# Token-shift mixes built in PSUM instead of SBUF, and all their low parts on VectorE

## The chip, the cores and the metric

The kernel runs on one core of a Trainium2 chip. The metric is the device time of one launch, in microseconds (us). A run before the change takes 3714.47 us, the median of three. TensorE (PE), VectorE (DVE), ScalarE (ACT), GpSimd (POOL) and SyncE (SP, which here only issues DMAs) run side by side and meet through semaphores.

## The reference

The program is a two-layer encoder trunk over 1024 tokens of width 1024: layer 0 is attention, layer 1 an RWKV-7 time mixing, and each layer has a squared-ReLU MLP. The change lies at the start of layer 1:

```python
dx_p = jnp.pad(h, ((0, 0), (1, 0), (0, 0)))[:, :-1] - h      # previous token minus this one
dx_n = jnp.pad(h, ((0, 0), (0, 1), (0, 0)))[:, 1:] - h       # next token minus this one
def mix(c):
    return h + dx_p * mu_prev[c] + dx_n * mu_next[c]
xw, xa, xg = mix(1), mix(4), mix(5)
r = mix(0) @ w_r
k = mix(2) @ w_k
v = mix(3) @ w_v
# and, for each direction d: tanh(xw @ w1[d]), xa @ a1[d], sigmoid(xg @ g1[d])
```

A mix is thus a weighted sum of a token and its two neighbours, with weights per channel; six mixes feed six groups of projections.

## The kernel before

Layer 1's input lies in SBUF as `u` (channels on partitions in 8 tiles `kt`, tokens along the free dimension, one column of zeros at either end). Work goes by halves of 512 tokens. Products are made in three passes of a split format: each operand is cut into a high part (fp32r) and a low part (what is left), and `mm3` multiplies high by high, high by low and low by high into one PSUM bank. So each `mix` of one channel tile and one half (128 x 512) is five instructions:

1. ACT writes `x = u * c0` (L884), c0 being one minus both weights;
2. and 3. DVE adds the previous and the next token, each times its weight, in place in `x` (L886, two instructions);
4. ACT rounds `x` to the high part `xh` (L890; the tile is `xmh` or `xsh`);
5. DVE, or POOL for c = 5 and c = 1, subtracts: `xl = x - xh` (L891).

`x` comes from pool `p0`, three buffers in SBUF. `stream` runs over the 8 channel tiles: a mix, the load of the weight tile `wr`, its high part on ACT (L904), its low part on POOL (L905), then the matmuls. `together` takes turns between streams. The stage that the change touches is the block under `es_h`. For each half it runs the first four output tiles of r beside the gate's hidden layer (c = 5), then the other four (which use the same mixes, kept in `px`) beside the hidden layers of c = 1 and c = 4. That is 4 x 8 mixes a half, 64 in all, and 576 matmuls of 512 columns. The projections of k and v (c = 2 and c = 3) follow under `es_a` and after it, with 32 more mixes, beside work of the second low-rank layers.

The kernel uses PSUM as 8 banks of 128 x 512 f32. In the `es_h` stage four belong to `r_pm` (r's sums) and one each to `s0` and `s1` (the hidden layers' sums); two are free. Before the stage all 8 banks are the MLP's ring `pm` (six in a left-hand pool, two in a right-hand one, taken in turn; the MLP's last transposes use it too). After it, `es_a` takes four banks (`s0` three, `s1` one).

A scheduler of the framework orders the instructions of each engine when the program is built, by the order in which they are written and by what its own clock says is ready; each engine then runs its list strictly in order. Nothing in the stage is ordered by hand.

## Time and profile before

| | |
|---|---|
| median of 3 runs | 3714.47 us (3712.27 to 3717.64) |
| the profiled execution: time, span | 3712.8 us, 3710.7 us |
| PE, DVE, ACT, POOL busy, share of the span | 86%, 70%, 50%, 50% |
| mean granted clock of TensorE | 0.904 |

The time of the profiled execution is 2.1 us above its span, which runs from the first to the last instruction. A busy share is a mean over stages that have different limits, so the stage has to be read by itself. Matmuls overlap one another, so that the sum of their times is more than the time that they need.

### The profile page before, as it was taken

How to read it: one execution, taken by the hardware profiler on the slowest of the kernel's cores; microseconds unless marked ns; L12 is line 12 of the kernel's file. 1: busy time of each engine (PE TensorE's matmuls, PEld its weight loads, DVE VectorE, ACT ScalarE, POOL GpSimd, SP SyncE). 2: the span in 40 equal slices, each digit the busy share in tenths (PEclk: the TensorE clock that was granted, in tenths of full speed). 3: DMA queues.
4: the chain of work that ended last, by engine and by line, in shares of the span. 5: the costliest groups of instructions: out<-in, count | busy, mean ns of one | idle time of the engine just before them, and what ended most of it. 6: DMA issues, size and time to landing. Idle time of an engine off the chain costs nothing. (4 is left out here: it accounts for less than half of the span.)

```text
span 3710.7 us, 61321 instructions
## 1 busy us (share of the span) xinstructions
PE 3197.8 (86%) x22168; PEld 2599.8 (70%) x22168; DVE 2596.9 (70%) x4617; ACT 1854.2 (50%) x4244; POOL 1850.4 (50%) x1642
## 2 busy tenths in 40 slices
PE   7999989799998978878888687787787889999998
PEld 6788987688777755555566575666666667887776
DVE  3355564744599979986963678888886565449996
ACT  2366564455543345654533365556566445554333
POOL 1000001655598877754566434444331146558887
PEclk9999999899999989879987587788787899999999
DMA  6222224232322032248766444444443413223023
GB/s 199 71 78 88 70 74 153 92 118 103 108 91 114 12 127 74 82 143 230 230 209 189 112 111 112 111 122 120 119 109 114 137 65 148 106 80 142 28 87 114
DMA packets 425100, 425.70 MB, mean 115 GB/s; under 512 B 138667, under 2 KB 338475, under 8 KB 418652
## 3 DMA queue, kind: packets, MB, share of 16 engines
q1 hardware_dynamic: 423612, 417.58, 36.3%
q0 software_dynamic: 1184, 4.20, 0.4%
q8 instruction: 174, 2.85, 0.3%
q14 instruction: 130, 1.06, 0.1%
HBM read 290.83 MB, written 138.20 MB: 116 GB/s over the span
## 5 line engine op out<-in xcount | busy, mean ns | idle before, releaser
L101 PE MATMUL pm<-bhi,lo 128*128 128x512 f32 x840 | 333.1, 399 | 46.3 <-DVE lo L130 46.1
L130 DVE TENSOR_TENSOR lo<-x,hi 128x512 fp32r<-128x512 f32 x300 | 322.1, 1080 | 61.8 <-ACT hi L129 61.7
L129 ACT ACTIVATE hi<-x 128x512 fp32r<-128x512 f32 x300 | 189.6, 633 | 323.4 <-DVE x L127 126.5
L100 PE MATMUL pm<-blo,hi 128*128 128x512 f32 x840 | 331.8, 395 | 8.6 <-POOL blo L130 8.1
L99 PE MATMUL pm<-bhi,hi 128*128 128x512 f32 x840 | 320.5, 394 | 5.4 <-ACT bhi L129 5.0
L127 POOL TENSOR_TENSOR x<-w1r 128x512 f32<-128x512 f32 x160 | 214.0, 1341 | 202.1 <-DVE lo L130 178.1
L130 POOL TENSOR_TENSOR blo<-bx,bhi 128x512 fp32r<-128x512 f32 x138 | 222.3, 1612 | 26.6 <-ACT bhi L129 26.0
L1270 POOL TENSOR_TENSOR af<-af,amask 128x512 f32<-128x512 f32 x128 | 163.8, 1286 | 136.7 <-ACT af L1269 111.9
L101 PEld LDWEIGHTS pm<-bhi,lo 128*128 128x128 f32 x840 | 158.4, 189 | 99.1 <-DVE lo L130 67.6
L905 POOL TENSOR_TENSOR wl<-wr,wh 128x512 fp32r<-128x512 f32 (+2 forms) x144 | 188.8, 1322 | 77.1 <-ACT wh L904 57.1
L1266 PE MATMUL A<-zr,bk 128*128 128x128 f32 x1024 | 187.4, 346 | 44.3 <-DVE bk L1259 38.1
L127 POOL TENSOR_TENSOR bx<-w 128x512 f32<-128x512 f32 x140 | 215.5, 1541 | 9.5
L886 DVE SCALAR_TENSOR_TENSOR x<-u,mu,x 128x512 f32<-128x512 f32 x192 | 208.4, 1121 | 7.9 <-ACT x L884 5.7
L1266 PEld LDWEIGHTS A<-zr,bk 128*128 128x128 f32 x1024 | 166.5, 249 | 58.6 <-POOL bk L1260 21.0
L127 DVE TENSOR_TENSOR x<-h 128x512 f32<-128x512 f32 x140 | 195.5, 1408 | 5.3 <-ACT h L268 2.7
L100 PEld LDWEIGHTS pm<-blo,hi 128*128 128x128 f32 x840 | 159.0, 189 | 49.5 <-POOL blo L130 16.0
L99 PEld LDWEIGHTS pm<-bhi,hi 128*128 128x128 f32 x840 | 159.3, 190 | 38.9 <-ACT bhi L129 5.9
L99 PE MATMUL mm<-xmh,wh 128*128 128x512 f32 x384 | 168.5, 460 | 17.0 <-ACT xmh L890 6.5
L1418 PE MATMUL c<-af,sv 128*64 128x64 f32 x1024 | 97.5, 275 | 79.8 <-DVE h L1412 71.2
L100 PE MATMUL mm<-xml,wh 128*128 128x512 f32 x384 | 157.1, 412 | 7.6 <-DVE xml L891 7.6
L1412 DVE SCALAR_TENSOR_TENSOR h<-c,pc,hd 64x64 f32<-64x64 f32 x448 | 126.8, 283 | 47.9 <-PE c L1403 30.3
L583 ACT ACTIVATE S<-S,mneg 128x256 f32<-128x256 f32 (+2 forms) x256 | 125.2, 501 | 67.0 <-DVE mneg L578 44.1
(370 smaller groups left out, 10044.3 us busy)
## 6 DMA issues: line engine op xcount, KB each, us to landing
w1r<-in_mlp_w_dram SPq DMA_DIRECT2D x32, 1024.0 KB, 5.4
w<-in_mlp_w_dram SPq DMA_DIRECT2D x32, 1024.0 KB, 5.5
x<-x SPq DMA_DIRECT2D x64, 386.0 KB, 3.4
hd<-h SPq DMA_DIRECT2D x24, 1024.0 KB, 4.2
h<-hd SPq DMA_DIRECT2D x24, 1024.0 KB, 7.8
wr<-in_w_rkv_dram SPq DMA_DIRECT2D x96, 256.0 KB, 2.8
rk<-rk SPq DMA_DIRECT2D x64, 256.0 KB, 3.9
x<-cs SPq DMA_DIRECT2D x32, 260.0 KB, 3.9
```

The source lines that it names most:

```text
L99: nc.tensor.matmul(out, lhsT=ahi, rhs=bhi, start=start, stop=False)
L100: nc.tensor.matmul(out, lhsT=ahi, rhs=blo, start=False, stop=False)
L101: nc.tensor.matmul(out, lhsT=alo, rhs=bhi, start=False, stop=stop)
L127: add.tensor_tensor(out=y, in0=x, in1=blocks[term[2]], op=ALU.add if term[1] == "+" else ALU.subtract)
L129: nc.scalar.activation(hi, x, AF.Copy)
L130: sub.tensor_tensor(out=lo, in0=x, in1=hi, op=ALU.subtract)
L583: nc.scalar.activation(s[:, :n], s[:, :n], AF.Exp, bias=mneg[:, i:i + 1], scale=-1.0)
L886: nc.vector.scalar_tensor_tensor(out=x, in0=at(2 * i), scalar=mu[:, i, c, kt:kt + 1], in1=x, op0=ALU.mult, op1=ALU.add)
L905: nc.gpsimd.tensor_tensor(out=wlo, in0=wr, in1=whi, op=ALU.subtract)
L1266: nc.tensor.matmul(ps[:, fsl(u, P)], lhsT=bk[:, u, j].rearrange("p a b -> p (a b)"), rhs=zr[:, u].rearrange("p a b -> p (a b)"), start=Tru ...
L1270: nc.gpsimd.tensor_tensor(out=o, in0=o, in1=consts["amask"].unsqueeze(1).to_broadcast([P, 4, P]), op=ALU.mult)
L1412: nc.vector.scalar_tensor_tensor(out=hn[rows, cols], in0=ch[rows, 128:192], scalar=pc[rows, u:u + 1], in1=hd[rows, cols], op0=ALU.mult, op ...
```

## The change

For the `es_h` stage alone, `x` is a PSUM tile: a pool of two banks is opened with `s0` and `s1`, and removed from the table before the stages of k and v, whose mixes find the SBUF pool `p0` again. And the subtraction that makes the low part is on DVE for every mix; c = 5 and c = 1 (32 of the 64 mixes) had it on POOL. The arithmetic is the same.

```diff
@@ mix
-            x = p0.tile([P, 512], F32, tag="x", name="x")
+            x = psd.get("x", p0).tile([P, 512], F32, tag="x", name="x")
             nc.scalar.activation(x, at(1), AF.Copy, scale=c0[:, c, kt:kt + 1])
...
-            (nc.gpsimd if c in (5, 1) else nc.vector).tensor_tensor(out=xl, in0=x, in1=xh, op=ALU.subtract)
+            nc.vector.tensor_tensor(out=xl, in0=x, in1=xh, op=ALU.subtract)
@@ under es_h
-            psd.update({n: pool(f"r_p{n}", 1, st=es_h, space=PSUM) for n in ("s0", "s1")})
+            psd.update({n: pool(f"r_p{n}", b, st=es_h, space=PSUM) for n, b in (("s0", 1), ("s1", 1), ("x", 2))})
             for half in range(2):
                 together(main(0, 0, half, 0, r_done(half)), gate_hidden(5, half))
                 together(main(0, 0, half, 1, r_done(half)), hidden(1, 0, half), hidden(4, 1, half))
+            del psd["x"]
```

## Rows read from the trace of the kernel before

**Rows 1.** The page: the span, then busy time, share and instructions of each engine.

```profile
span 3710.7 us, 61321 instructions
PE 3197.8 (86%) x22168; PEld 2599.8 (70%) x22168; DVE 2596.9 (70%) x4617; ACT 1854.2 (50%) x4244; POOL 1850.4 (50%) x1642
```

**Rows 2.** Busy time of each engine from 1381 to 1588 us, the stage of the change (the end of the MLP's last tiles at its left edge): stretch, its length, PE, weight loads, DVE, ACT, POOL (busy us, instructions), granted clock, DMA share, GB/s.

```profile
1381.00:1588.00 207.00, 162.09 (x592) 115.74 (x592) 197.50 (x182) 124.21 (x237) 148.88 (x117) 0.90 0.25 82
```

**Rows 3.** DVE's groups in the same stretch: line, operation, shapes, count, busy us, mean ns of one, idle before them and what ended it.

```profile
L886 DVE SCALAR_TENSOR_TENSOR x<-u,mu,x 128x512 f32<-128x512 f32 x132 | 147.5, 1160 | 7.2 <-ACT x L884 5.7
L891 DVE TENSOR_TENSOR xml<-x,xmh 128x512 fp32r<-128x512 f32 x16 | 20.9, 1308 | 0.2
L891 DVE TENSOR_TENSOR xsl<-x,xsh 128x512 fp32r<-128x512 f32 x16 | 17.9, 1132 | 0.0
L988 DVE TENSOR_TENSOR sg<-th,sg 128x512 fp32r<-128x512 f32 x4 | 4.8, 1207 | 0.1
...
L976 DVE CAST ta<-th 64x512 fp32r<-64x512 f32 x2 | 0.8, 422 | 0.0
```

**Rows 4.** L886, and L891 on DVE with `xml` as its output, over the whole span: count, then the shortest, median and longest in ns, first and last start.

```profile
L886 DVE SCALAR_TENSOR_TENSOR x<-u,mu,x x192: 719/833/1852, 1381.2 to 1943.9; 128x512 f32<-128x512 f32 x192
L891 DVE TENSOR_TENSOR xml<-x,xmh x48: 676/693/1786, 1390.4 to 1946.5; 128x512 fp32r<-128x512 f32 x48
```

**Rows 5.** Timelines of DVE and of POOL around 1445 us: start, length, what.

```profile
1443.65 0.74 DVE L886 SCALAR_TENSOR_TENSOR x<-u,mu,x 128x512 f32<-128x512 f32 x1
1444.31 0.68 DVE L988 TENSOR_TENSOR sg<-th,sg 128x512 fp32r<-128x512 f32 x1
...
1446.47 1.68 DVE L988 TENSOR_TENSOR sg<-th,sg 128x512 fp32r<-128x512 f32 x1
...
1444.41 1.74 POOL L905 TENSOR_TENSOR wl<-wr,wh 128x512 fp32r<-128x512 f32 x1 [2.15 <-DVE x L886]
1446.12 1.48 POOL L891 TENSOR_TENSOR xsl<-x,xsh 128x512 fp32r<-128x512 f32 x1
```

**Rows 6.** A stretch of layer 0's MLP, 1100 to 1300 us. First the engines' busy times as in rows 2; then L335, whose second input `pm` is a PSUM bank (shortest, median, longest); then a group of the same stretch with both inputs in SBUF.

```profile
1100.00:1300.00 200.00, 180.04 (x771) 143.01 (x771) 199.31 (x201) 75.56 (x131) 169.41 (x110) 1.00 0.15 58
L335 DVE TENSOR_TENSOR acc<-acc,pm x92: 672/674/677, 1099.6 to 1288.3; 128x512 f32<-128x512 f32 x92
L130 DVE TENSOR_TENSOR lo<-x,hi 128x512 fp32r<-128x512 f32 x44 | 62.3, 1431 | 0.0
```

**Rows 7.** Scalar-tensor-tensor instructions of DVE over the whole span: L1047 with its second tensor `sm` in PSUM, L806 with its first in PSUM (`mm`) and with both in SBUF (`y`), and L73, which is 1024 wide (shortest, median, longest).

```profile
L1047 DVE SCALAR_TENSOR_TENSOR kk<-k,par,sm x16: 733/734/748, 1641.0 to 1878.1; 128x512 f32<-128x512 f32 x16
L806 DVE SCALAR_TENSOR_TENSOR y<-mm,prs,grow x24: 740/743/752, 604.8 to 3012.8; 128x512 f32<-128x512 f32 x24
L806 DVE SCALAR_TENSOR_TENSOR y<-y,prs,grow x8: 743/744/752, 588.4 to 2941.0; 128x512 f32<-128x512 f32 x8
L73 DVE SCALAR_TENSOR_TENSOR un<-xt,rs,ngrow x8: 1283/1284/1286, 18.0 to 80.0; 128x1024 f32<-128x1024 f32 x8
```

**Rows 8.** How closely such instructions follow one another: DVE's timeline at 1641 us (start, length), and one piece of the chain that ended last, six instructions of L335 in a row.

```profile
1640.96 0.74 DVE L1047 SCALAR_TENSOR_TENSOR kk<-k,par,sm 128x512 f32<-128x512 f32 x1
1641.62 0.75 DVE L886 SCALAR_TENSOR_TENSOR x<-u,mu,x 128x512 f32<-128x512 f32 x1
...
3409.85 3.58 DVE acc L335 x6
```

**Rows 9.** ACT's groups from 1381 to 1588 us, as in rows 3.

```profile
L884 ACT ACTIVATE x<-u,c 128x512 f32<-128x512 f32 x64 | 45.3, 720 | 33.5 <-POOL xsl L891 12.8 <-DVE xml L891 11.7 <-DVE xsl L891 8.8
L890 ACT ACTIVATE xsh<-x 128x512 fp32r<-128x512 f32 x48 | 30.1, 628 | 26.6 <-DVE x L886 26.3
L904 ACT ACTIVATE wh<-wr 128x512 fp32r<-128x512 f32 x33 | 20.4, 619 | 5.2 <-PE mm L100 4.4 <-DMA wr<-in_w_rkv_dram 0.8
L904 ACT ACTIVATE wh<-wr 128x128 fp32r<-128x128 f32 x32 | 9.6, 298 | 0.5 <-POOL wl L905 0.3 <-PE mm L100 0.2
L904 ACT ACTIVATE wh<-wr 128x256 fp32r<-128x256 f32 x16 | 6.5, 405 | 0.0
```

**Rows 10.** PE: the first and the last of 26 matmuls in a row (start, length), and what PE's idle time before the stage's matmuls ended with, from 1381 to 1588 us (us, times).

```profile
1396.11 0.39 PE L99 MATMUL mm<-xmh,wh 128*128 128x512 f32 x1
...
1401.88 0.40 PE L100 MATMUL mm<-xsl,wh 128*128 128x512 f32 x1
  DVE xsl L891: 18.5, 13
  POOL wl L905: 14.0, 23
...
  DVE xml L891: 11.9, 8
```

**Rows 11.** The edges of the stage. ACT's timeline: the last copies of the MLP's transposes out of its PSUM banks (L837) and the stage's first writes of `x`; PE's timeline: a wait at the first matmuls; and the first matmul of `es_a` into its own banks, over the whole span.

```profile
1375.77 0.59 ACT L837 ACTIVATE u<-pm 128x512 f32<-128x512 f32 x1
1378.25 1.95 ACT L884 ACTIVATE x<-u,c 128x512 f32<-128x512 f32 x3
1393.97 0.59 ACT L837 ACTIVATE u<-pm 128x512 f32<-128x512 f32 x1
1394.61 0.19 PEld L99 LDWEIGHTS mm<-xmh,wh 128*128 128x128 f32 x1 [1.54 <-ACT u L837]
L1088 PE MATMUL sm<-sg,g2h x64: 388/396/796, 1608.4 to 1910.0; 128*128 128x512 f32 x64
```

## The prediction, made before the change was run

> **What bounds the kernel now.** I read the page's first part for the whole [rows 1], then only the stage of the change, because a share of the span says nothing about a stage. From 1381 to 1588 us DVE is busy 197.5 of 207.0 us; PE's 162.1 us are overlapped matmuls, ACT has 124.2 and POOL 148.9 [rows 2]. PE's need is smaller than it looks: 26 matmuls start between 1396.11 and 1401.88 us, 0.231 us apart, so 576 need 133 us [rows 10]. What ends PE's idle time is mostly the low parts on DVE (18.5 and 11.9 us), then the weights' low parts on POOL. DVE bounds this stage, and the stage bounds the kernel while it lasts, since k, v and the scan come behind it.

> Next, why DVE is that busy. L886 takes 1160 ns on average in the stage [rows 3], but 719 at its shortest and 1852 at its longest [rows 4]: same work, more than twice the time. The two timelines around 1445 us show the pattern [rows 5]. At 1443.65 us, POOL idle, L886 takes 0.74. At 1444.31 L988 starts a moment before POOL's next subtraction and takes 0.68, while POOL's takes 1.74. At 1446.47 L988 starts after a POOL subtraction has begun (1446.12, 1.48 long), and now it takes 1.68. Whichever starts second waits for the other. All of these read two tensors from SBUF.

> The decisive rows are from another stage. From 1100 to 1300 us DVE is busy 199.3 of 200.0 us and POOL 169.4, so they run against each other all the time. There L130, with two SBUF inputs, takes 1431 ns on average, and L335, of the same size but with one input in PSUM, takes 672 to 677 in 92 instances [rows 6]. One input out of SBUF ends the collision. The scalar-tensor-tensor form shows the same: 733 to 748 ns with one tensor in PSUM (L1047) [rows 7], against 719 for an undisturbed L886 [rows 4].

> **The change, part by part.** I count DVE by the distance from one start to the next, since neighbours overlap a little: an L886 starts 0.66 us after an L1047 of 0.74, and six L335 fill 3.58 us, 0.58 to 0.60 apiece [rows 8]. Values: 0.66 for L886, 0.60 for a low part.

> (1) `x` in PSUM. Each of the 128 L886 then has one tensor in SBUF and one in PSUM: 128 x 0.66 = 84.5 us. No row shows DVE writing PSUM. From below, the write costs nothing; from above, I let reading and writing one bank halve the rate: 512 more elements take 1284 - 743 = 541 ns [rows 7], so 1.20 us each, 153.6 in all. I take the lower end, since L1047 and L806, which differ from the new form only in where the result goes, are nearest. (2) Low parts: 64 x 0.60 = 38.4 us, the 32 taken over from POOL among them; they have a PSUM input too. (3) The rest stays: the group's eight small lines, 18.3 us (first and last in rows 3), and four L886 that already belong to k, 4.6.

> Sum: 84.5 + 38.4 + 18.3 + 4.6 = 145.8 us against 197.5, so 51.7 us less work on DVE. Moving 32 subtractions to DVE alone would cost 19 us; it is paid for by the collisions that it ends.

> [...]

> (4) The ring of `x` shrinks from three buffers to two, and this is where I give some back. DVE must not be late, yet L884 may overwrite a bank only after the low part (L891) has read it. L884 (0.72 us, rows 9) then waits on ACT, and queued behind it stand the high part L890 of the other mix and the weights' high parts L904; for L890 DVE's next low part and PE wait. If ACT's order is good, L884 runs under the other mix's second L886 and is late by 0.72 + 0.04 - 0.66, some 0.1 us a mix, 6 us in all. L904 needs 36 us on ACT in the stage [rows 9]; I let a quarter of it, 9 us, fall in front of an L884. So 15 us more idle time on DVE than the 9.5 of now. From below it is nothing (k's first mixes, in their own SBUF ring, can fill holes); the upper bound is the first rival. (5) ACT's own work stays (124 of some 170 us), POOL loses its 32 subtractions, PE's 133 us remain under DVE's 145.8. No DMA moves; the weight loads on SP's queue only come sooner, at a DMA share of 0.25 [rows 2].

> (6) The edges. Taken in turn, the `pm` ring ends so that `x` gets the two right-hand banks, whose copies are done by about 1376.4 us, before L884's first write at 1378.25; r's banks are those that PE waits for until 1394.6 already [rows 11]. At the end, `es_a` reuses `x`'s banks first at 1608 us or later, 20 us after the stage's last mix. Both cost nothing.

> Net: 51.7 - 15 = 36.7 us. Against the profiled execution's own 3712.8 us (1.7 below the median of the runs) this gives **3676 us**. Its own range, from no added idle time to twice what I took, plus some 8 us for a list that the scheduler orders anew, is 3655 to 3695.

> **The rivals.** First: *the two-bank ring sets the pace.* If ACT's list has the next L884 in front of the other mix's L890, DVE does a low part, then waits a whole L884 and its hand-over (0.77 us) in every mix: 64 x 0.77 = 49 us idle in place of 15, and 51.7 - 49 leaves 2.7: 3710 us. For it: ACT already waits 33.5 us in front of L884 with three buffers [rows 9]. Against: those waits are on a DVE that is late by collisions, and the program's order puts L890 ahead.

> Second, the other side: *in-place work in PSUM is slow.* At 1.20 us an L886, DVE needs 153.6 + 38.4 + 22.9 = 214.9 us, 17.4 more than now: 3730 us. It turns to a loss from (84.5 + 51.7) / 128 = 1.06 us each. For it: no row shows it. Against: the reads alone cost nothing extra. Its mild form is a small fixed cost; the rows show at most the 14 ns between 719 and 733, 3 us in all.

> Third: *`x`'s banks are not free at the start*, and the mixes wait for the last copy at 1394.6 us instead of starting at 1378: DVE's first L886 comes 13 us later, 3689 us. Against it stands the order of the ring.

> Fourth: *the time goes elsewhere.* PE waits as long for POOL's and ACT's weight parts, or the lists behind the stage come out worse by as much as this one gains: 3705 to 3714 us. For it: POOL's `wl` holds PE for 14.0 us already [rows 10]; against: POOL loses work.

> **How the numbers follow.** Forecast 0.69; ring 0.09; slow PSUM 0.08; late start 0.08; elsewhere 0.06. A difference under 0.2% (7.4 us) is about what a measurement of this kernel can not tell from none. Faster: the forecast, the late start, half of the ring and of the last case: 0.84. Same: the other halves, with a mild form of slow PSUM: 0.08. Slower: slow PSUM, and a little for lists ordered badly: 0.08. For 8 in 10 the range takes the forecast's range and the late start, most of the ring and of the last case: 3653 to 3709 us.

> **What would show each step right or wrong.** L886 in the stage should read 730 to 760 ns with hardly any spread, L891 some 680, all 64 of the stage on DVE; either above 1 us and the second rival holds. The stage, from the first L886 to k's first, should last some 170 us in place of 207. DVE's idle time in front of L886, ended by ACT's `x`, should be near 20 us; near 50 it is the ring. POOL's `wl` of 128 x 512 should fall from its present length, as DVE no longer holds it up. An L886 that starts only at 1395 us shows the late start. Wrong I'd be above all if the stage shortened and the end didn't: then the span behind 1620 us has grown.

## The result and the profile after

The changed kernel takes 3667.36 us (median of 4 runs, 3666.84 to 3671.37) against 3714.28 us in the runs beside it: a ratio of 0.9883, 95% interval 0.987 to 0.9896. The forecast was 3676 us, with a range of 3653 to 3709. The sign and the mechanism were right, and the stage became shorter as foretold; the gain is 46.9 us where the sum gave 36.7.

The page's first part of the changed kernel, in answer to [rows 1]:

```profile
span 3665.6 us, 61287 instructions
PE 3183.3 (87%) x22168; PEld 2592.9 (71%) x22168; DVE 2533.5 (69%) x4649; ACT 1849.0 (50%) x4244; POOL 1772.7 (48%) x1610
```

DVE has 32 instructions more and is busy 63 us less; POOL has 32 fewer and is busy 78 us less. PE's count is the same.

The stage of the change, from 1381 us to 1559 us (r's last copy starts at 1557.1 us; before it was 1592.5; two of the stage's low parts start behind that edge), as in [rows 2] (busy us and instructions of PE, weight loads, DVE, ACT, POOL):

```profile
1381.00:1559.00 178.00, 152.73 (x591) 114.32 (x592) 164.23 (x235) 131.57 (x253) 75.11 (x85) 0.91 0.31 102
```

DVE's and POOL's main groups in that stretch, in answer to [rows 3]:

```profile
L886 DVE SCALAR_TENSOR_TENSOR x<-u,mu,x 128x512 f32<-128x512 f32 x147 | 108.3, 777 | 8.6 <-ACT x L884 6.7
L891 DVE TENSOR_TENSOR xsl<-x,xsh 128x512 fp32r<-128x512 f32 x46 | 31.4, 687 | 2.4 <-ACT xsh L890 1.5
L891 DVE TENSOR_TENSOR xml<-x,xmh 128x512 fp32r<-128x512 f32 x24 | 17.2, 716 | 0.9 <-ACT xmh L890 0.7
...
L905 POOL TENSOR_TENSOR wl<-wr,wh 128x512 fp32r<-128x512 f32 x33 | 44.1, 1336 | 59.7 <-ACT wh L904 53.3 <-PE mm L101 3.8 <-PE mm L99 2.5
L905 POOL TENSOR_TENSOR wl<-wr,wh 128x128 fp32r<-128x128 f32 x32 | 16.3, 511 | 38.6 <-ACT wh L904 18.6 <-PE mm L101 14.4 <-PE mm L99 2.8
```

POOL's same two groups before the change, from 1381 to 1588 us:

```profile
L905 POOL TENSOR_TENSOR wl<-wr,wh 128x512 fp32r<-128x512 f32 x33 | 50.8, 1538 | 26.0 <-ACT wh L904 20.3 <-PE mm L100 3.2 <-DVE x L886 2.2
L905 POOL TENSOR_TENSOR wl<-wr,wh 128x128 fp32r<-128x128 f32 x32 | 27.1, 850 | 8.0 <-issue 5.1 <-ACT wh L904 2.3 <-PE mm L100 0.4
```

L886 fell from 1160 to 777 ns, L891 from 1132 and 1308 to 687 and 716. POOL gained too: its 128 x 512 subtraction of the weights fell from 1538 to 1336 ns and its 128 x 128 one from 850 to 511 (means). DVE's timeline around 1445 us and POOL's under it, in answer to [rows 5]; a row with x4 merges four neighbours, and can hold several shapes under the name of one:

```profile
1442.89 2.88 DVE L886 SCALAR_TENSOR_TENSOR x<-u,mu,x 128x512 f32<-128x512 f32 x4
1446.00 1.29 DVE L891 TENSOR_TENSOR xsl<-x,xsh 128x512 fp32r<-128x512 f32 x2 [0.23 <-ACT xsh L890]
...
1443.54 0.46 POOL L905 TENSOR_TENSOR wl<-wr,wh 128x128 fp32r<-128x128 f32 x1 [1.66 <-ACT wh L904]
1445.36 1.71 POOL L905 TENSOR_TENSOR wl<-wr,wh 128x512 fp32r<-128x512 f32 x2 [1.36 <-ACT wh L904]
```

Four L886 fill 2.88 us, 0.72 apiece, while POOL works under them, and two L891 fill 1.29, 0.65 apiece. No DVE instruction here is stretched beside POOL, as L988 was in [rows 5].

One thing in these rows is not the change's own: there are 147 L886 in the stretch, and the stage has only 128. At least 19 of them, and eight of the L891 (24 write `xml`, where r has 16; e5's expectation below says six), belong to the first mixes of k. They use the SBUF ring, which `x` has left free, and DVE does them among the stage's own. They still collide: the longest L886 of the stretch takes 1753 ns, and without k's mixes (e5) none is above 758.

To see where the time went, I follow a few marks through the program. All are starts in us from the beginning of the span, read from one trace of each kernel: r's last copy out of PSUM, k's last copy, the last `y` of v on POOL (end of the projections), the last matmul `c<-af,sv` of the scan, and the span. The last two columns are differences of these: the scan's length, from v to `c`, and what follows it.

| kernel | r | k | v | c | span | v to c | c to end |
|---|---|---|---|---|---|---|---|
| before | 1592.5 | 1827.0 | 1997.1 | 2908.8 | 3710.7 | 911.7 | 801.9 |
| changed | 1557.1 | 1787.0 | 1953.8 | 2862.7 | 3665.6 | 908.9 | 802.9 |
| e1 low parts alone | 1576.4 | 1813.4 | 1981.5 | 2893.1 | 3694.8 | 911.6 | 801.7 |
| e2 one bank | 1638.1 | 1871.0 | 2040.2 | 2966.1 | 3773.3 | 925.9 | 807.2 |
| e3 no POOL | 1529.7 | 1769.0 | 1939.3 | 2859.6 | 3669.9 | 920.3 | 810.3 |
| e4 POOL twice | 1566.2 | 1794.6 | 1963.1 | 2887.7 | 3693.0 | 924.6 | 805.3 |
| e5 k held | 1541.9 | 1785.8 | 1955.9 | 2842.4 | 3645.3 | 886.5 | 802.9 |
| e6 MLP too | 1539.3 | 1771.7 | 1942.0 | 2865.2 | 3648.7 | 923.2 | 783.5 |
| e7 no POOL, two buffers | 1539.9 | 1784.3 | 1953.2 | 2883.5 | 3689.6 | 930.3 | 806.1 |
| e8 k held, MLP too | 1527.6 | 1768.2 | 1937.7 | 2844.9 | 3626.3 | 907.2 | 781.4 |
| e9 before, k held | 1593.1 | 1829.0 | 1997.0 | 2909.6 | 3713.3 | 912.6 | 803.7 |

For the change: 35.4 us at r's end, 40.0 at k's end, 43.3 at v's end, 45.1 at the end of the span. So nearly all of it is earned in front of the scan. r's last copy isn't the stage's last work, though: the hidden layers' low parts (`xsl`) go on behind it. Before the change, in the changed kernel and in e5, which holds k's first mixes back, they run on DVE (count, shortest, median, longest in ns, first and last start):

```profile
L891 DVE TENSOR_TENSOR xsl<-x,xsh x16: 678/942/1783, 1439.7 to 1584.5; 128x512 fp32r<-128x512 f32 x16
L891 DVE TENSOR_TENSOR xsl<-x,xsh x48: 675/691/693, 1392.7 to 1562.4; 128x512 fp32r<-128x512 f32 x48
L897 DVE TENSOR_TENSOR xsl<-x,xsh x48: 676/691/694, 1390.0 to 1543.7; 128x512 fp32r<-128x512 f32 x48
```

By this mark the changed kernel is only 22.1 us ahead, but has eight mixes of k behind it already; e5, without them, is 40.8 us ahead.

The table also carries a warning that the experiments below need: the scan's code is the same in every kernel, and its length still lies between 886 and 930 us. TensorE's granted clock (the last column but two) differs with it, here in e5's scan, the shortest, and in e7's, the longest:

```profile
1955.90:2842.40 886.50, 693.17 (x10536) 570.61 (x10536) 679.51 (x1851) 512.63 (x1672) 363.56 (x443) 0.78 0.47 119
1953.20:2883.50 930.30, 719.36 (x10534) 592.54 (x10534) 697.48 (x1851) 514.03 (x1671) 363.37 (x443) 0.74 0.44 113
```

No run separates the two, the clock and the order of the instructions; and runs of one kernel differ by up to 15 us (e9, 3712.7 to 3728.1). Conclusions are therefore drawn from marks in front of the scan first, and from end times only where they agree.

### The profile page after: what moved, and what is told of

Its sections match the earlier page's. It is cut to its first block, busy times and chain, and to the rows that moved or that the text cites. A ratio compares the mean times of both kernels' runs of the same rounds, so it can differ in the third digit from the quotient of the medians.

```text
span 3665.6 us, 61287 instructions
## 1 busy us (share of the span) xinstructions
PE 3183.3 (87%) x22168; PEld 2592.9 (71%) x22168; DVE 2533.5 (69%) x4649; ACT 1849.0 (50%) x4244; POOL 1772.7 (48%) x1610
## 5 line engine op out<-in xcount | busy, mean ns | idle before, releaser
L130 DVE TENSOR_TENSOR lo<-x,hi 128x512 fp32r<-128x512 f32 x300 | 322.0, 1079 | 63.3 <-ACT hi L129 63.1
L127 POOL TENSOR_TENSOR x<-w1r 128x512 f32<-128x512 f32 x160 | 214.5, 1344 | 201.6 <-DVE lo L130 178.2
L130 POOL TENSOR_TENSOR blo<-bx,bhi 128x512 fp32r<-128x512 f32 x138 | 222.8, 1615 | 25.3 <-ACT bhi L129 25.0
L905 POOL TENSOR_TENSOR wl<-wr,wh 128x512 fp32r<-128x512 f32 (+2 forms) x144 | 160.1, 1123 | 127.8 <-ACT wh L904 92.7
L127 POOL TENSOR_TENSOR bx<-w 128x512 f32<-128x512 f32 x140 | 215.9, 1544 | 9.5
L1267 PEld LDWEIGHTS A<-zr,bk 128*128 128x128 f32 x1024 | 166.5, 250 | 59.8 <-POOL bk L1261 22.1
L127 DVE TENSOR_TENSOR x<-h 128x512 f32<-128x512 f32 x140 | 195.9, 1410 | 5.3 <-ACT h L268 2.7
L886 DVE SCALAR_TENSOR_TENSOR x<-u,mu,x 128x512 f32<-128x512 f32 x192 | 153.9, 834 | 9.2 <-ACT x L884 6.7
L335 DVE TENSOR_TENSOR acc<-acc,pm 128x512 f32<-128x512 f32 x256 | 158.1, 675 | 0.0
```

Source lines behind the costliest of these rows:

```text
L127: add.tensor_tensor(out=y, in0=x, in1=blocks[term[2]], op=ALU.add if term[1] == "+" else ALU.subtract)
L130: sub.tensor_tensor(out=lo, in0=x, in1=hi, op=ALU.subtract)
L335: dve.tensor_tensor(out=a, in0=a, in1=banks[j], op=ALU.add if sign == "+" else ALU.subtract)
L886: nc.vector.scalar_tensor_tensor(out=x, in0=at(2 * i), scalar=mu[:, i, c, kt:kt + 1], in1=x, op0=ALU.mult, op1=ALU.add)
L905: nc.gpsimd.tensor_tensor(out=wlo, in0=wr, in1=whi, op=ALU.subtract)
L1267: nc.tensor.matmul(ps[:, fsl(u, P)], lhsT=bk[:, u, j].rearrange("p a b -> p (a b)"), rhs=zr[:, u].rearrange("p a b -> p (a b)"), start=Tru ...
```

## The experiments

### e1: all low parts on DVE, x left in SBUF

```diff
-            (nc.gpsimd if c in (5, 1) else nc.vector).tensor_tensor(out=xl, in0=x, in1=xh, op=ALU.subtract)
+            nc.vector.tensor_tensor(out=xl, in0=x, in1=xh, op=ALU.subtract)
```

> The second half of the change alone: all low parts on DVE, x still in SBUF with three buffers. Theory (DVE and POOL block one another whenever a DVE instruction reads two SBUF tensors, and x in PSUM is what ends it): POOL keeps its 81 subtractions of weights, so of the some 71 us that DVE loses to collisions in the stage (128 x 0.425 on L886 and 17 on the low parts) about 81/113, 51 us, stay, and 32 low parts of 0.60 us come on top: DVE's work is again some 196 us and the time 3706 to 3722 us, about that of before; L886 averages 0.95 to 1.1 us. Rival (POOL's slow low parts were the trouble, where x lies makes no difference): as fast as the whole change, 3665 to 3680 us.

3706.36 us (median of 8), ratio 0.9967, interval 0.9955 to 0.9979: at the lower edge of what the theory had. The stage's DVE groups from 1381 to 1576 us:

```profile
L886 DVE SCALAR_TENSOR_TENSOR x<-u,mu,x 128x512 f32<-128x512 f32 x134 | 129.2, 1007 | 2.2 <-ACT x L884 1.8
L891 DVE TENSOR_TENSOR xsl<-x,xsh 128x512 fp32r<-128x512 f32 x48 | 38.7, 820 | 0.0
```

And the stretch as in [rows 2]:

```profile
1381.00:1576.00 195.00, 157.88 (x595) 115.71 (x595) 190.53 (x216) 127.64 (x246) 106.71 (x88) 0.89 0.30 94
```

L886 is at 1007 ns as the theory has it, and DVE is busy 190.5 of 195 us. In the trace the end of the projections moves by 15.6 us, but the traced execution is the fastest of the eight (3696.57 us); the median moves by 8.8. So the moved low parts are worth something even with `x` in SBUF, where 32 POOL instructions fewer are there to collide with: 15.6 of 43.3 us by the marks, 8.8 of 46.9 by the medians, from under a fifth to over a third. The rest came with `x`'s place.

### e3: no work for POOL in the stage, x in SBUF

The low part of the weights is not computed in the stage; the high part is multiplied in its place, so that the matmuls are as many as before. This is built on e1.

```diff
-                wlo = pw.tile([P, 512], F32R, tag="wl", name="wl")[:, :n * P]
                 nc.scalar.activation(whi, wr, AF.Copy)
-                nc.gpsimd.tensor_tensor(out=wlo, in0=wr, in1=whi, op=ALU.subtract)
+                wlo = whi
+                if not stage[0]:
+                    wlo = pw.tile([P, 512], F32R, tag="wl", name="wl")[:, :n * P]
+                    nc.gpsimd.tensor_tensor(out=wlo, in0=wr, in1=whi, op=ALU.subtract)
```

> x in SBUF with three buffers and all low parts on DVE as in e1, and POOL left without work in the stage: the low part of the weights is not computed there, the high part is multiplied twice (as many matmuls as before). Theory (collisions): with POOL silent L886 takes 0.72 to 0.75 us with x in SBUF too, the stage is as short as with the whole change, and the time is 3655 to 3672 us. Rival (PSUM is faster for these instructions by itself, POOL or not): L886 stays above 0.9 us and the time above 3690 us.

3673.84 us, ratio 0.9882 (0.9867 to 0.9897), 1.8 us above the theory's range. The group of L886 (L887 in this numbering) from 1381 to 1530 us:

```profile
L887 DVE SCALAR_TENSOR_TENSOR x<-u,mu,x 128x512 f32<-128x512 f32 x132 | 92.9, 754 | 4.4 <-ACT x L885 3.6
```

Its shortest, median and longest in the same stretch:

```profile
L887 DVE SCALAR_TENSOR_TENSOR x<-u,mu,x x132: 737/746/1752, 1381.1 to 1529.4; 128x512 f32<-128x512 f32 x132
```

And the stretch:

```profile
1381.00:1530.00 149.00, 139.87 (x590) 111.47 (x590) 139.31 (x213) 122.58 (x237) 3.21 (x5) 0.96 0.37 118
```

With POOL silent the same instruction, on the same SBUF tiles as before, takes 754 ns instead of 1160. That the collision is the cause is thereby shown, and that PSUM is not faster for this instruction by itself: e5's, on PSUM tiles, takes 752 ns. r's last copy comes 62.8 us earlier than before (1529.7), more than in the changed kernel. The time doesn't show it, since the scan and what follows came out 9 and 8 us longer than before. PE is now busy 139.9 of 149 us, near the 133 that the prediction reckoned for 576 matmuls.

### e4: POOL's work doubled, x in PSUM

```diff
-                nc.gpsimd.tensor_tensor(out=wlo, in0=wr, in1=whi, op=ALU.subtract)
+                for _ in range(2 if "x" in psd else 1):
+                    nc.gpsimd.tensor_tensor(out=wlo, in0=wr, in1=whi, op=ALU.subtract)
```

> The whole change with twice the work on POOL: in the stage the subtraction for the low part of the weights is done two times over (81 more instructions, some 73 us; POOL then has about 148 us in the stage, as many as before the change). Theory (with one input in PSUM DVE no longer meets POOL): L886 and L891 stay at their 0.75 and 0.69 us, DVE's busy time in the stage stays at some 164 us, and the time grows only by what PE waits longer for the weights, 3667 to 3685 us. Rival (the gain came from the lower load on POOL): L886 back above 0.95 us, 3695 us or more.

3698.52 us, ratio 0.9946 (0.9931 to 0.9961): the time lies where the rival had it. The trace says otherwise. L886 from 1381 to 1568 us:

```profile
L886 DVE SCALAR_TENSOR_TENSOR x<-u,mu,x 128x512 f32<-128x512 f32 x147 | 111.5, 792 | 7.0 <-ACT x L884 5.2
```

Its shortest, median and longest in the same stretch:

```profile
L886 DVE SCALAR_TENSOR_TENSOR x<-u,mu,x x147: 734/750/1829, 1382.0 to 1567.9; 128x512 f32<-128x512 f32 x147
```

And the stretch:

```profile
1381.00:1568.00 187.00, 154.13 (x595) 111.13 (x596) 172.05 (x236) 131.20 (x253) 148.41 (x166) 0.93 0.31 96
```

POOL is busy 148.4 us, just as before the change (148.9 in [rows 2]), and L886 takes 792 ns, not the 950 or more of the rival. The median is 750, against 751 in the changed kernel's stretch with half of POOL's work: L886 on a PSUM tile doesn't meet POOL. What lifts the mean above it are most likely k's mixes in SBUF, which are in this stretch too. r's last copy comes 9.1 us later than in the changed kernel, within what the theory allowed for the weights, and v 9.3 us later. The other 18 of the 27 us between the two spans arise behind v: the scan takes 924.6 us in place of 908.9, and what follows 2.4 more. My expectation left that out and missed by it.

### e2: one bank for x

```diff
-... for n, b in (("s0", 1), ("s1", 1), ("x", 2))
+... for n, b in (("s0", 1), ("s1", 1), ("x", 1))
```

> The whole change with one PSUM bank for x in place of two. Theory (DVE's work is the limit with two banks, and the chain of a mix with one): a mix then takes its whole chain, 0.69 + 0.66 + 0.75 + 0.60 + 0.68 us and five hand-overs of 0.04, 3.6 us, 64 of them 230 us in place of some 170: 3715 to 3740 us. If the ring already sets the pace with two banks, one bank doubles the stage's length: above 3800 us. If it costs nothing: 3667 us.

3776.13 us, ratio 1.0161 (1.0144 to 1.0178), and r's last copy comes 81.0 us later than in the changed kernel. DVE's groups from 1381 to 1640 us (the idle time before each group is behind the bar):

```profile
L886 DVE SCALAR_TENSOR_TENSOR x<-u,mu,x 128x512 f32<-128x512 f32 x144 | 110.6, 778 | 44.5 <-ACT x L884 41.7
L891 DVE TENSOR_TENSOR xsl<-x,xsh 128x512 fp32r<-128x512 f32 x45 | 31.0, 690 | 32.1 <-ACT xsh L890 30.6 <-PE mm L100 0.7 <-PE mm L101 0.7
```

The instructions are as short as with two banks; the gaps are not: 44.5 us in front of L886 against 8.6, 32.1 in front of L891 against 2.4. With one bank the chain of a mix sets the pace, and the change would have lost what it gained and more. The time lies 36 us above my range of 3715 to 3740. Some 20 of these are the stage (81 us later, where I had reckoned 60), a difference that I didn't follow up; the rest is mostly the scan, 925.9 us, 17 longer than the changed kernel's.

### e7: e3 with two buffers for x

The weights' low part is left out as in e3; the ring of `x` in SBUF has two buffers, behind the stage too.

```diff
-        p0 = pool("r_m", 3)
+        p0 = pool("r_m", 2)
```

> e3 (x in SBUF, POOL without work in the stage, the weights' low part left out there and the high part multiplied twice) with two buffers for x in place of three, in the stages of k and v too. It prices the shorter ring by itself, without collisions. My prediction gave the ring 15 us. Theory: r's last copy comes 5 to 15 us later than e3's 1529.7 us, and the time is 3678 to 3692 us. Rival 1 (the ring is free with two): 1530 us and 3672 to 3676 us. Rival 2 (the ring sets the pace): 1570 us or later, above 3710 us.

3688.7 us, ratio 0.9925 (0.991 to 0.994). r's last copy comes at 1539.9 us, 10.2 us later than with three buffers, and v's end 13.9 us later; both ranges held. The stage's last low part (`xsl`, L892) starts at 1549.4 us against 1530.1 in e3, 19.3 us later. So the shorter ring costs 10 to 19 us in SBUF with POOL silent, by the mark that one takes.

### e5: k's first mixes held back

```diff
+        low = [None]
         def mix(c, kt, half, p, tag, bufs):
+            with (tc.issue_after(low[0]) if c == 2 and half == 0 else ExitStack()):
+                return mix_(c, kt, half, p, tag, bufs)
+        def mix_(c, kt, half, p, tag, bufs):
...
-            nc.vector.tensor_tensor(out=xl, in0=x, in1=xh, op=ALU.subtract)
+            i = nc.vector.tensor_tensor(out=xl, in0=x, in1=xh, op=ALU.subtract)
+            if "x" in psd:
+                low[0] = i.ins
```

> The whole change, but the DVE instructions of k's first eight mixes (c = 2, half 0) are put behind the stage's last low part in DVE's order. In the changed kernel 19 of their additions and 6 of their subtractions run inside the stage, from the free SBUF ring. Theory (k's mixes fill DVE's gaps there, and what r loses by them k gets back): r's last copy comes some 10 to 20 us earlier than 1557 us, k's first copy 3 to 9 us later against 1583 us, and the time is 3668 to 3678 us. Rival (k's mixes are only in r's way): both come earlier and the time falls below 3662 us.

3651.28 us, ratio 0.9822 (0.9807 to 0.9837). Here the stage holds its own mixes and no others. L886 (L892 in this numbering) from 1381 to 1540 us, shortest, median and longest:

```profile
L892 DVE SCALAR_TENSOR_TENSOR x<-u,mu,x x125: 739/752/758, 1381.8 to 1539.2; 128x512 f32<-128x512 f32 x125
```

Its group:

```profile
L892 DVE SCALAR_TENSOR_TENSOR x<-u,mu,x 128x512 f32<-128x512 f32 x125 | 89.1, 752 | 8.0 <-ACT x L890 5.6
```

And the stretch:

```profile
1381.00:1540.00 159.00, 145.42 (x586) 111.59 (x586) 142.78 (x205) 121.61 (x233) 70.76 (x84) 0.93 0.34 106
```

All 125 lie between 739 and 758 ns, while POOL is busy 70.8 us beside them. r's last copy comes at 1541.9 us, within 2 us of e7's 1539.9: `x` in two PSUM banks beside a working POOL is worth as much as `x` in two SBUF buffers with POOL silent. As the theory had it, r comes 15.2 us earlier than in the changed kernel. k's first copy comes at 1576.9 us, 5.7 us earlier than there (1582.6), where the theory had it 3 to 9 us later: at this mark the rival was right. The lead shrinks to 1.2 us at k's last copy and is gone at v's end (2.1 us later): what k's hoisted mixes take from r, the projections get back by their end. The time fell 17 us below the range all the same, and all of that lies behind v, in a scan of 886.5 us (the traced execution is 4 us under the median). So it is below the rival's 3662 us without the rival's reason, since nothing of k's lead is left at v's end. Neither theory explains the scan.

### e9: the kernel before, with e5's edit

```diff
+            with (tc.issue_after(low[0]) if c == 2 and half == 0 else ExitStack()):
...
+            if c == 4:
+                low[0] = i.ins
```

> The kernel before, with the edit of e5 alone: DVE's instructions of k's first eight mixes stand behind the last low part of c = 4. Before the change only four of them run inside the stage, so that the order there hardly changes; what changes is that the framework's scheduler lays out everything behind it anew. It asks how much of a difference of end times is due to the lists behind the stage. Theory (the scan's length depends on the list that comes out, by some 20 us either way, whatever was changed in front): the last y of v within 4 us of 1997 us, and from there to the end anything between 1690 and 1733 us instead of 1714, time 3688 to 3735 us. Rival (e5's gain behind the stage comes from holding k): from there to the end about 1690 us as in e5, 3685 to 3692 us. Rival 2: the lists behind it have no such weight: 1712 to 1716 us, 3711 to 3719 us.

3718.8 us (median of 10), ratio 1.0005 (0.9995 to 1.0016), and a scan of 912.6 us. Rival 2's time came out, and the rival that holding k shortens the scan by itself is refuted here; e8, which holds k too, has a scan of 907.2 us. The theory is neither shown nor refuted by this run, since one more list with an unchanged length says little. For it stand the scans of the table, 886 to 930 us with the same code; but the granted clock differed among them as well, and what makes one scan longer than another stays open.

### e6 and e8: the same idea in the MLPs

The stretch of [rows 6] has the same trouble: DVE busy 199.3 of 200 us, and its low parts of the first factor at 1431 ns beside a busy POOL. Their `x` is written by DVE itself, so it can lie in PSUM. Two banks are taken from the ring of the products, which then has six, and the sums are taken out bank by bank.

```diff
-            factor(nc, Seven.A[m], ab, mj.x, *a, dve, dve)
+            factor(nc, Seven.A[m], ab, lambda: ps[1].tile([P, 512], F32, tag="pm", name="ax"), *a, dve, dve)
...
-                banks = [pm() for _ in range(4)]
+                banks = [ps[0].tile([P, 512], F32, tag="pm", name="pm") for _ in range(4)]
...
-            for i, sign in Seven.TO[m]:
-                for j in range(4):
+            for j in range(4):
+                for i, sign in Seven.TO[m]:
```

> The whole change, and the same idea in the second product of both MLPs, where DVE is busy 98 to 99% and POOL 84%: the sums that DVE builds for the first factor lie in two PSUM banks in place of SBUF, so that their low part reads one tensor from SBUF; the products' own ring shrinks from eight banks to six there, and the banks are taken bank by bank. From the changed kernel's rows: some 60 low parts of 1.44 us in each MLP would take 0.68, 45 us less on DVE in each; but PE is busy about 90% there and POOL 84%, so at most 10% of two stretches of 290 us: 20 to 50 us, if the shorter ring of banks does not hold PE up. Theory: 3620 to 3650 us. Rival (six banks make PE wait at every change of group, 21 in each MLP): slower than the whole change, 3675 us or more.

3652.77 us, ratio 0.9829 (0.9811 to 0.9847): 2.8 us above the theory's range, and well under the rival's. From 1100 to 1300 us, in answer to [rows 6]:

```profile
1100.00:1300.00 200.00, 189.76 (x804) 151.45 (x803) 176.75 (x211) 80.18 (x142) 174.40 (x122) 0.98 0.19 72
```

Two of DVE's groups there:

```profile
L127 DVE TENSOR_TENSOR ax<-h 128x512 f32<-128x512 f32 x43 | 53.2, 1244 | 1.2
L130 DVE TENSOR_TENSOR lo<-ax,hi 128x512 fp32r<-128x512 f32 x44 | 29.9, 682 | 10.6 <-ACT hi L129 9.6 <-PE pm L100 1.0
```

And the sum in front of it as it was before, with its result in SBUF:

```profile
L127 DVE TENSOR_TENSOR x<-h 128x512 f32<-128x512 f32 x45 | 58.5, 1313 | 0.7
```

The low part takes 682 ns where it took 1431; the sum (L127), which reads two SBUF tensors and now writes to PSUM, still takes 1244 where it took 1313. So it is the inputs that count, not where the result goes. DVE is busy 176.8 us in place of 199.3, and PE 189.8 in place of 180.0. Layer 1's MLP and what follows (c to end) takes 783.5 us instead of 802.9, and layer 0's ends some 21 us earlier (the first additions of its last tiles start at 1301.9 us against 1322.7). Of these 40 us the span shows 17: the projections took 9 us and the scan 14 us longer than in the changed kernel.

e8 puts e5 and e6 together.

> e5 and e6 together: the whole change, k's first mixes held back on DVE, and the first factor's sums of both MLPs' second product in PSUM. In front of the scan e6 brought some 12 us and behind the scan 22 more, e5 nothing in front of the scan: the last y of v at 1940 to 1946 us, the last MLP some 22 us shorter than in the changed kernel, the scan unknown within 45 us: 3605 to 3655 us. If both gains add up as the times read (16 and 15 us): 3636 us.

3631.91 us, ratio 0.9776 (0.9756 to 0.9797): 35 us under the changed kernel and within what was expected. v ends at 1937.7 us, 2 us ahead of the expected range. It beats both kernels.

## Why the prediction was right, point by point

**The bound** (DVE, by collisions with POOL): right. e3 takes POOL's work away and e4 doubles it; L886 goes to 754 ns in the one with `x` in SBUF, and stays at 792 (median 750) in the other with `x` in PSUM. Beside a working POOL, L886 takes 1160 ns in the stage with both its tensors in SBUF (before), and 752 with one of them in PSUM (e5).

**Term 1, 128 L886 at 0.66 us from start to start**: right within a tenth. In place in one PSUM bank, the form that no row of before showed, it takes 739 to 758 ns in e5, against 719 at best in SBUF. The four in a row of the changed kernel fill 2.88 us, some 0.71 from start to start, by which 128 would take 91 us, not 84.5; three in a row a little later are as close as forecast, 2.07 us for the three, 0.66 from start to start:

```profile
1448.45 2.07 DVE L886 SCALAR_TENSOR_TENSOR x<-u,mu,x 128x512 f32<-128x512 f32 x3 [0.24 <-ACT x L884]
```

The second rival, in-place work at half the rate, is refuted. Of its mild form, a small fixed cost, the traces show 6 ns at most: e3's SBUF form with POOL silent has a median of 746 ns and a mean of 754, e5's PSUM form a median and a mean of 752.

**Term 2, 64 low parts at 0.60**: right, 687 to 690 ns on average where L335 had 672 to 677. **The sum**, 145.8 us of DVE, 4.6 of them for k: e5, the kernel whose stage is purest, has 142.8 up to 1540 us, and three L886 and two low parts of the stage, some 3 us, behind that edge.

**Term 4, the ring of two** was the step that I mis-sized: 15 us of added idle time on DVE. Measured are 13.8 us of idle time in the changed kernel's stage and 16.2 in e5's, against 9.5 before: 4 to 7 us added. In front of L886, where I said near 20 us ended by ACT's `x`, there are 6.7. e7 puts the ring in SBUF at 10 to 19 us, around the 15 that I took, but DVE in these two kernels lost less. Why they lost less is open. ACT's copies became shorter too (below), by some 4 us in all over 64 mixes; k's mixes in the gaps, which I had named but counted at nothing, explain little, since e5 without them idles only 2.4 us more.

**The length of the stage**, some 170 us from the first L886 to k's first, can't be read in the changed kernel, where k's first mixes lie inside the stage. In e5, from its first L886 (1381.8 us) to its last low part (1543.7), it is 162 us.

**The edges**: right. L884 first writes `x` at 1378.6 us, where it was 1378.25, and the first `xsl` starts on DVE at 1392.7, where it was 1391.0 on POOL; the late start didn't come. **The first rival**, the two-bank ring as the pace, is refuted by the small gaps, and e2 shows what it looks like when it is true.

**Where the remainder comes from.** The sum of 36.7 us was meant for a stage without k's mixes. The changed kernel's gain is 22.1 us at the stage's last low part, 35.4 at r's end and 43.3 at v's end; what comes after the stage is k's, whose first mixes were done by then. e5, without them, has 40.8, 50.6 and 41.2 us at the same three marks, so that the two kernels agree only at v's end. Taken there, the mis-sized term accounts for the difference: with the 4 to 7 us that were measured in the place of 15, the sum gives 45 to 47 us, against 43.3 in the changed kernel. That is an account by sums, not by a run that varies the term alone. What the scan adds, 2.8 us, and the part behind it takes, 1.0, lies far inside the spread that the table shows for them, and I count it to nobody.

**The fourth rival**, in its form that the lists behind the stage come out worse, didn't happen to this change. But five of the experiments (e2, e3, e4, e6, e7) have scans 11 to 21 us longer than the changed kernel's, and e5 one that is 22 us shorter; whether by their lists or by the granted clock isn't shown. I gave the rival 0.06 and 8 us of the range; the table says that such an allowance was too narrow. That the end landed 9 us from the forecast owes something to luck there.

## What to carry to other kernels

Where DVE and POOL are both busy and DVE's times spread between one and two and a half times their shortest, look at which of its instructions read two tensors from SBUF: here putting one of the two in a free PSUM bank ended the waiting of these instructions (L886 from 1160 ns to 752) and shortened POOL's (128 x 512 from 1538 ns to 1336), and cost next to nothing even in place (752 ns against 754 with POOL silent). Keep two banks for such a tile; one bank turned the gain into a loss (ratio 1.0161). And where a scheduler lays out the whole program anew, judge an edit by marks in front of the code that it doesn't touch: here an unchanged scan moved by more than 40 us, as much as the change itself, for a reason that stayed open.

## What the runs showed of the hardware beyond that

- ACT's copies were 4 to 5% shorter with PSUM on either side. In e5's stage, where at most three of the 63 can be k's, L884 (L890 in its numbering) took 691 ns on average writing to PSUM against 720 writing to SBUF [rows 9], and L890 (L896) 596 reading from PSUM against 628:

```profile
L890 ACT ACTIVATE x<-u,c 128x512 f32<-128x512 f32 x63 | 43.1, 691 | 14.2 <-DVE xsl L897 7.2 <-DVE xml L897 5.9
L896 ACT ACTIVATE xsh<-x 128x512 fp32r<-128x512 f32 x46 | 27.0, 596 | 4.5 <-DVE x L892 3.5
```
